# Transposes in place of identity matmuls for the input combinations, and a value group's weight sums on GpSimd

## The chip, the cores and the metric

The kernel runs on one core of a Trainium2 chip. The metric is the device time of one execution in microseconds (us). The profile is of one execution, taken by the hardware profiler. Engines are named as it names them: PE (TensorE matmuls), PEld (its weight loads), DVE (VectorE), ACT (ScalarE), POOL (GpSimd) and SP (SyncE, which issues most DMAs here). L389 is line 389 of the kernel.

## The reference

One encoder layer with two parallel gated branches is applied to two batches with the same weights: `x_prompt` (1024 rows of 1024) and `x_sample` (512 rows). The change touches the very first step for `x_prompt` alone, the normed input and its product with the columns of the input projection that give the values and the gates:

```python
def encoder_layer(x, pre_w, w_in, conv_w, conv_b, i_bias, f_bias, head_norm_w, w_pm, w_pa, w_out, post_w, rel_table):
    b_, s_, _ = x.shape
    h = rms_norm(x, pre_w)
    cols = jnp.einsum('bsd,dc->bsc', h, w_in)
    m_qk, m_v, m_o, m_z, m_i, m_f, a_qkv, a_z, gate = jnp.split(cols, np.cumsum(IN_SPLITS)[:-1], axis=-1)
    ...
    return x + rms_norm(out, post_w)
```

All is float32. What follows (a bidirectional mLSTM, dilated window attention, gated merge and output projection) is not touched.

## The kernel before

**How float32 products are made.** A float32 operand is split into a high part (rounded by an ACT copy to the matmul's faster float32 form) and a low part (DVE: value minus high part). `mm3` (L209 to L211) then makes a product of three matmuls: high by high, and the two mixed ones.

**Winograd's form of Strassen's product.** For `x_prompt` the product of input and weights is done as a two by two block product with seven block products in place of eight. The rows fall into two halves of 512 (i = 0, 1) and the 1024 input columns into two halves; `combos` (L372) calls the four blocks a0, b0 (first rows) and a1, b1 (second rows). The seven left operands are named B11, T2, B21, T3, T1, T4, B22, and kept turned (input column on the partitions) in `H[0][m]` (high) and `H[1][m]` (low), four tiles of 128x512 each. With the normed blocks: B11 = a0, B21 = b0, B22 = b1, T1 = a1 - a0, T2 = b1 - a1 + a0, T3 = b1 - a1 and T4 = b0 - b1 + a1 - a0, that is b0 - T2.

**One value group** (`value_group`, L454) covers 644 columns of the weights: `va` and `vb` hold the upper and lower half of the weights' rows, `vsum` the sums. `sums` (L444) makes three of them on DVE, 128x1288 each: vb0 + vb1, va0 - vb0 (which takes the place of vb0) and vsum0 - va0. `split` makes the high and low part of one right operand (`vhi` on ACT, L477; `vlo` on DVE, L478), into two places used in turn. `product` runs 48 matmuls of 128x322 in four groups of twelve, and between the groups it steps through a generator (`with_m1`, `with_m2`, `with_m7`, `with_m6`) in which the first group (g = 0) makes the left operands while PE multiplies. So the order on PE is written out by hand: products m1 (B11), m2 (B21), m7 (T3), m6 (T2), m5 (T1), m4 (T4), m3 (B22), and between them the puts.

**A put** (`put`, L419) makes tile k of operand m: PE turns four 128x128 blocks into one PSUM bank; ACT copies it to the high part (L432); the low part is DVE's subtraction (L434), but for B21 and B22 a matmul by the negative identity `minus` takes the high part off in PSUM (`rest`, L438) and ACT copies what is left (L439). Which blocks are turned is in `terms`: one block with the identity for B21, B22, T1 and T2 (for B21 and B22 as a plain float32 matmul, for the others as a transpose), and two blocks for T3 and T4, where the second is a plain float32 matmul by the negative identity. A plain float32 matmul of 128x128 shows as two passes in the trace, a transpose as one.

**What else runs then.** DVE norms the rows (L410, 128x512, the row block times its root and the norm weights; sixteen of them behind one another for b0, b1, a1, a0) and makes T1 and T2 in place of a0 and b1 (`sub`, L415 and L417). POOL makes the roots (L297 to L298, L406 to L407) and one half of the first low part. ACT copies the gate columns of finished value tiles (L503, `gall`) after DVE has added them up (L594, into `u2b`). DVE, ACT and POOL run their instructions in the order in which the scheduler put them; `issue_after` adds an order, and `high_priority` lets `split` go ahead. The rows and weights of the first group come by SP's queue at the start; for the groups 1 to 3 `value_group` loads `va` and `vb` as their places come free, and the results leave by SP's queue through `vz` (three places, L509 and L510).

**The later units** (`unit_pair`, L693) use the same seven left operands for the other columns.

Of the kernel before, what the change touches and what calls it, by code (L numbers as in the profile page):

```python
# [22 lines left out]
F32 = mybir.dt.float32  # L23
F32R = mybir.dt.float32r
AF = mybir.ActivationFunctionType
# [4 lines left out]
P = 128  # L30
# [15 lines left out]
VW = 322  # L46
# [135 lines left out]
class Net:  # L182
# [32 lines left out]
    def put(self, key, out, src, of, queue=None, lag=None):  # L215
        if self.defer:
            self.pending.append((self.clock + (lag or self.lag), key, (out, src), self.owner.get(id(of))))
        else:
            (queue or self.nc.sync).dma_start(out, src)
# [149 lines left out]
            self.nc.scalar.mul(self.cw[:, c], self.cw[:, c], x)  # L369


    def combos(self, ps, H, xt, r, junk, pw, minus, again, diag):  # L372

        nc = self.nc
        part = lambda i, j: [x[:, j * BLK:(j + 1) * BLK] for x in xt[i]]  # L380
        a0, b0, a1, b1 = part(0, 0), part(0, 1), part(1, 0), part(1, 1)
        plus, neg = self.ident, minus.bitcast(F32)
        terms = {B21: [(b0, plus)], B22: [(b1, plus)], T3: [(b1, plus), (a1, neg)],
                 T1: [(a0, plus)], T2: [(b1, plus)], T4: [(b0, plus), (b1, neg)]}

        def lead():
            ps_ = [ps.tile([P, BLK], F32, name="d") for _ in range(4)]
            for t in range(4):
                nc.vector.tensor_scalar(diag[t], self.ident, self.root(xt[0][t], r[t], junk), None, op0=OP.mult)  # L389
                for k in range(4):  # L390
                    nc.tensor.matmul(ps_[k][:, t * P:(t + 1) * P], a0[t][:, k * P:(k + 1) * P], diag[t], start=t == 0,
                                     stop=True, skip_group_check=True)
            for k in range(4):
                hi, lo, w = H[0][B11][:, k], H[1][B11][:, k], self.prew[:, k:k + 1]
                self.high = nc.scalar.activation(hi, ps_[k], AF.Copy, scale=w)
                self.low = nc.vector.scalar_tensor_tensor(lo, ps_[k], w, hi.bitcast(F32), op0=OP.mult, op1=OP.subtract)  # L396

        roots = {}

        def norm(i, t, j):  # L400

            if i and j and t % 2 == 0:
                two = r[4 + t // 2].rearrange("p (a b) -> p a b", a=3)
                for a in range(2):
                    nc.scalar.activation(junk, xt[i][t + a], AF.Square, accum_out=two[:, 0, a:a + 1])
                nc.gpsimd.tensor_scalar(two[:, 1], two[:, 0], 1.0 / D, EPS, op0=OP.mult, op1=OP.add)  # L406
                nc.gpsimd.tensor_tensor(two[:, 2], two[:, 1], self.mhalf, op=OP.pow)  # L407
                roots.update({t: two[:, 2, :1], t + 1: two[:, 2, 1:]})
            x, c = xt[i][t], slice(j * BLK, (j + 1) * BLK)
            return nc.vector.scalar_tensor_tensor(x[:, c], x[:, c], roots[t] if i else r[t][:, 2:3], pw[:, c], op0=OP.mult, op1=OP.mult)  # L410

        def sub(m):
            for t in range(4):
                if m == T1:
                    nc.vector.tensor_sub(a0[t], a1[t], a0[t])  # L415
                else:
                    nc.vector.tensor_sub(b1[t], b1[t], a0[t])  # L417

        def put(m, k):  # L419

            if m == T4 and k == 0:
                again()
            p = ps.tile([P, BLK], F32, name="d")
            for t in range(4):
                for i, (x, one) in enumerate(terms[m]):
                    of, to = x[t][:, k * P:(k + 1) * P], p[:, t * P:(t + 1) * P]
                    if i == 0 and m not in (B21, B22):
                        nc.tensor.transpose(to, of, one)
                    else:
                        nc.tensor.matmul(to, of, one, start=t == i == 0, stop=True, skip_group_check=True)  # L430
            hi, lo = H[0][m][:, k], H[1][m][:, k]
            nc.scalar.activation(hi, p, AF.Copy)  # L432
            if m not in (B21, B22):
                self.low = nc.vector.tensor_sub(lo, p, hi.bitcast(F32))  # L434
                return None

            def rest():
                nc.tensor.matmul(p, minus, hi, start=False, stop=True, skip_group_check=True)  # L438
                nc.scalar.activation(lo, p, AF.Copy)  # L439
            return rest  # L440

        return lead, norm, sub, put

    def sums(self, wa, wb, s):  # L444

        nc = self.nc
        nc.vector.tensor_add(s[:, 0], wb[:, 0], wb[:, 1])
        nc.vector.tensor_sub(wb[:, 0], wa[:, 0], wb[:, 0])
        nc.vector.tensor_sub(s[:, 1], s[:, 0], wa[:, 0])

    def value_weights(self, sb):
        return [sb.tile([P, 2, 4 * VW], F32, name=x, bufs=1) for x in ("va", "vb", "vsum")]
# [1 line left out]
    def value_group(self, g, T, H, sb, us, co, ps, late=None, begin=None, u3=None, more=None, turn=None):  # L454
# [4 lines left out]
        nc = self.nc  # L459
# [61 lines left out]
        if g == 0:  # L521
# [44 lines left out]
            def with_m7():  # L566
                put(T1, 0), put(T1, 1)
                yield
                put(T1, 2), put(T1, 3)
                with self.tc.issue_after(low[1]):  # L570
                    sub(T2)
                yield
                put(T2, 0), put(T2, 1)
                yield
                put(T2, 2), put(T2, 3)
                low.append(self.low.ins)
                yield

# [6 lines left out]
            for t in range(4):  # L585
                nc.scalar.activation(u2[t], m1[t][:, :VW], AF.Copy)
            w12 = low.pop(0)
            with self.tc.issue_after(low[0]):
                self.sums(wa, wb, s)
            m2 = product(B21, w12, with_m2())  # L590
            held = []
            for t in range(4):
# [3 lines left out]
                sub(T1)  # L596
            m7 = product(T3, split(wb[:, 0]), with_m7())
            for t in range(4):
                add(u3[t], u2[t], m7[t][:, :VW])
            with self.tc.issue_after(low[1]):  # L600
                s2 = split(s[:, 1])
            m6 = product(T2, s2, with_m6())
# [5 lines left out]
            yield  # L608
            co = co()
        else:  # L610
            self.sums(wa, wb, s)
            m1 = product(B11, split(wa[:, 0], first))
            for t in range(4):
                nc.scalar.activation(u2[t], m1[t][:, :VW], AF.Copy)
            w12 = split(wa[:, 1])
# [15 lines left out]
            u3 = []  # L631
            for t in range(4):
                u3.append(tile_("u3", 4))
                add(u3[t], u2[t], m7[t][:, :VW])
            yield
        if g == 0:
            with self.tc.issue_after(low[2]):
# [55 lines left out]
    def unit_pair(self, weights, H, sb, cp, ps):  # L693
# [19 lines left out]
        nc.vector.tensor_add(q[0][0], u2, m2)  # L713
        nc.vector.tensor_add(u2, u2, m6)
        m7 = product(T3, s3)
        nc.vector.tensor_add(u3, u2, m7)
        m5 = product(T1, s1)
        nc.vector.tensor_add(q[1][1], u3, m5)
        nc.vector.tensor_add(u2, u2, m5)
# [1036 lines left out]
def body(tc, a):  # L1756
    N = Net(tc, a)
    nc = tc.nc
    (x1, y1), (x2, y2) = a["runs"]
    with ExitStack() as st:  # L1760
# [12 lines left out]
        with ExitStack() as s1:  # L1773
# [4 lines left out]
            with ExitStack() as sv:  # L1778
# [37 lines left out]
                def again():  # L1816
                    H[0][T4] = place("h", T4)

                turns = N.combos(ps, H, xt, r, H[1][T4][:, :2].rearrange("p a c -> p (a c)"), pw, minus, again, diag)
# [235 lines left out]
```

## Time and profile before

| | us |
|---|---|
| median of 3 runs (2253.35 to 2256.43) | 2254.23 |
| the profiled execution | 2252.45 |
| its span, first to last instruction | 2250.7 |
| PE busy in the span | 2238.9 |
| DVE busy | 1510.2 |
| ACT busy | 1128.0 |
| POOL busy | 713.5 |

A row of the time line gives the start and the length in us, engine, line, operation, output<-inputs, the shapes and how many instructions the row stands for; in brackets the idle time of the engine before it and what ended it. In a group's row "min/median/max" are lengths in nanoseconds. In a row of the waits stand the total, the number and the longest of the waits in us. A matmul's length overlaps the next one's, so that costs on PE are read from start to start. In the kernel's first 67 us the trace has 64 passes at L428, 64 at L430 by `minus` and 64 at L430 by the identity.

### The profile page before, as it was taken

How to read it: one execution, taken by the hardware profiler on the slowest of the kernel's cores; microseconds unless marked ns; L12 is line 12 of the kernel's file. 1: busy time of each engine (PE TensorE's matmuls, PEld its weight loads, DVE VectorE, ACT ScalarE, POOL GpSimd, SP SyncE). 2: the span in 40 equal slices, each digit the busy share in tenths (PEclk: the TensorE clock that was granted, in tenths of full speed). 3: DMA queues.
4: the chain of work that ended last, by engine and by line, in shares of the span. 5: the costliest groups of instructions: out<-in, count | busy, mean ns of one | idle time of the engine just before them, and what ended most of it. 6: DMA issues, size and time to landing. Idle time of an engine off the chain costs nothing.

```text
span 2250.7 us, 35392 instructions
## 1 busy us (share of the span) xinstructions
PE 2238.9 (99%) x12226; PEld 1964.4 (87%) x12226; DVE 1510.2 (67%) x2875; ACT 1128.0 (50%) x2369; POOL 713.5 (32%) x1000
## 2 busy tenths in 40 slices
PE   9999999999999999999999999999999999999998
PEld 8999888888888888888888899999888888888887
DVE  7765577687776665558887754544689854655674
ACT  6432244444443443457776655666665644554332
POOL 1000333333333222237676610011165522221221
PEclk9999999999999999999999999999999999999999
DMA  3652455543233223284664788997678897776663
GB/s 123 172 131 76 174 202 192 195 178 120 107 111 112 85 84 131 104 294 167 224 212 133 202 213 231 257 254 212 202 244 285 253 269 222 232 258 199 225 236 114
DMA packets 222685, 418.27 MB, mean 186 GB/s; under 512 B 24841, under 2 KB 128969, under 8 KB 222506
## 3 DMA queue, kind: packets, MB, share of 16 engines
q1 hardware_dynamic: 194536, 315.86, 44.3%
q0 software_dynamic: 24368, 87.56, 12.4%
q10 hardware_dynamic: 3602, 12.59, 1.4%
q8 instruction: 97, 1.59, 0.3%
q14 instruction: 82, 0.67, 0.1%
HBM read 296.19 MB, written 128.12 MB: 189 GB/s over the span
## 4 chain that ended last, share of the span: by engine, by line
PE 97%; issue 1%; DMA 1%; DVE 0%; ACT 0%; POOL 0%; DVEq 0%; POOLq 0%; ACTq 0%
PE d L211 14%; PE d L209 14%; PE d L210 14%; PE dense L209 12%; PE dense L211 12%; PE dense L210 12%; PE o L1400 4%; PE pt L1387 2%; PE lg L1364 2%; PE num L209 1%; PE num L211 1%; PE num L210 1%; PE a L1072 1%; PE kv L209 1%; PE kv L210 1%
## 5 line engine op out<-in xcount | busy, mean ns | idle before, releaser
L209 PE MATMUL dense<-H,wh 128*128 128x512 f32 x664 | 270.3, 407 | 0.0
L211 PE MATMUL dense<-H,wl 128*128 128x512 f32 x664 | 260.6, 393 | 0.0
L210 PE MATMUL dense<-H,wh 128*128 128x512 f32 x664 | 260.4, 392 | 0.0
L210 PE MATMUL d<-Hl,phla 128*128 128x512 f32 x608 | 236.5, 389 | 0.0
L211 PE MATMUL d<-Hh,phla 128*128 128x512 f32 x608 | 236.5, 389 | 0.0
L209 PE MATMUL d<-Hh,phla 128*128 128x512 f32 x608 | 236.5, 389 | 0.0
L278 DVE TENSOR_TENSOR wl<-wraw,wh 128x1024 fp32r<-128x1024 f32 (+1 forms) x121 | 149.5, 1236 | 66.4 <-ACT wh L272 66.3
L1376 DVE CUSTOM_DVE_ANT_0 ls<-lg,bias 128x256 f32<-128x256 f32 (+1 forms) x288 | 93.7, 362 | 135.2 <-PE lg L1364 69.8
L211 PE MATMUL d<-Hh,phlb 128*128 128x512 f32 x456 | 177.4, 389 | 0.0
L209 PE MATMUL d<-Hh,phlb 128*128 128x512 f32 x456 | 177.4, 389 | 0.0
L210 PE MATMUL d<-Hl,phlb 128*128 128x512 f32 x456 | 177.4, 389 | 0.0
L1380 ACT ACTIVATE ls<-ls,nm 128x256 f32<-128x256 f32 (+1 forms) x288 | 129.9, 452 | 83.3 <-DVE nm L1378 58.2
L687 POOL TENSOR_TENSOR psum_w<-pw_raw 128x512 f32<-128x512 f32 x38 | 55.0, 1447 | 366.0 <-DMA pw_raw<-w_in 222.5
L272 ACT ACTIVATE wh<-wraw 128x1024 fp32r<-128x1024 f32 (+1 forms) x124 | 128.5, 1037 | 72.4 <-PE dense L210 26.4
L211 PEld LDWEIGHTS dense<-H,wl 128*128 128x128 f32 x664 | 124.7, 188 | 28.1
L209 PE MATMUL d<-vhi,Hh 128*128 128x322 f32 x448 | 140.9, 314 | 0.3
L211 PE MATMUL d<-vhi,Hl 128*128 128x322 f32 x448 | 140.3, 313 | 0.4 <-DVE Hl L396 0.2
L210 PE MATMUL d<-vlo,Hh 128*128 128x322 f32 x448 | 139.6, 312 | 0.0
L210 PEld LDWEIGHTS dense<-H,wh 128*128 128x128 f32 x664 | 125.3, 189 | 14.3
L209 PEld LDWEIGHTS dense<-H,wh 128*128 128x128 f32 x664 | 125.0, 188 | 14.4
L209 PEld LDWEIGHTS d<-Hh,phla 128*128 128x128 f32 x608 | 114.1, 188 | 23.7
L210 PEld LDWEIGHTS d<-Hl,phla 128*128 128x128 f32 x608 | 114.1, 188 | 23.7
(570 smaller groups left out, 6158.5 us busy)
## 6 DMA issues: line engine op xcount, KB each, us to landing
pw_raw<-w_in SPq DMA_DIRECT2D x76, 512.0 KB
wraw<-w_in SPq DMA_DIRECT2D x64, 512.0 KB
aqk_a<-pwk SPq DMA_DIRECT2D x48, 512.0 KB
aqk_b<-sw SPq DMA_DIRECT2D x48, 256.0 KB
wraw<-w_pm POOLq DMA_DIRECT2D x24, 512.0 KB, 5.8
wraw<-w_out POOLq DMA_DIRECT2D x24, 512.0 KB, 3.9
wraw<-w_v POOLq DMA_DIRECT2D x22, 430.0 KB, 6.1
erep<-erow SPq DMA_DIRECT2D x16, 512.0 KB
```

Source lines behind the costliest of these rows:

```text
L209: nc.tensor.matmul(out, lh, rh, start=start, stop=False)
L210: nc.tensor.matmul(out, lh, rl, start=False, stop=False)
L211: nc.tensor.matmul(out, ll, rh, start=False, stop=stop)
L272: high = nc.scalar.activation(hi[:, :n], raw[:, :n], AF.Copy)
L278: low = (self.lows or nc.vector).tensor_sub(lo[:, :n], raw[:, :n], hi[:, :n].bitcast(F32))
L687: self.nc.gpsimd.tensor_add(s[:, 0], ws[1][:, 0], ws[1][:, 1])
L1072: nc.tensor.matmul(p[:, c - c0], kT[:, ct, c * P:(c + 1) * P], qT[:, ct, c * P:(c + 1) * P], start=ct == 0, stop=ct == 1)
L1364: nc.tensor.matmul(lg[:, hh, c:c + w], q[hh][:, qs], z[:, k0:k0 + w], start=z is k[hh], stop=z is not k[hh])
L1376: nc.vector.tensor_tensor_reduce(out=ls[:, hh], in0=ts["lg"][hh], in1=bt[:, hh], scale=1.0, scalar=NEG, op0=OP.add, op1=OP.max, accum_out= ...
L1380: self.held = self.held[-3:] + [nc.scalar.activation(ls[:, hh], ls[:, hh], AF.Exp, bias=nm[:, hh:hh + 1], accum_out=ot[:, 128 + hh:129 + hh])]
L1387: nc.tensor.transpose(pp[:, hh * nk + x], ts["ls"][:, hh, x * P:(x + 1) * P], self.ident)
L1400: nc.tensor.matmul(po[:, hh * 64:hh * 64 + 64], pt[:, hh * nk + x], v[:, kt[x], c0 + hh * 64:c0 + hh * 64 + 64], start=x == 0, stop=x == n ...
```

## The change

- `put` turns B21, B22, T1, T2 and now T3 (a1 alone) by transposes; the second block of T3 and all of T4 come from operands that are there already, by 128x512 matmuls with the identity or its negative: T3 = a1 - B22 (high and low, two matmuls), T4 = B21 - T2 (four matmuls, no transpose). T3 has the other sign than before, so that the results of its product are subtracted (also in `unit_pair`). A copy of the identity in the fast float32 form, `plus`, is made by ACT at the start.
- T2's puts stand one place earlier (one, two and one between the groups of m7 in place of two and two).
- The three sums of the first group go from DVE to POOL and no longer wait for the norms (`issue_after` is gone).
- In the later groups the split of `va` stands before the sums in the text.

```diff
-        plus, neg = self.ident, minus.bitcast(F32)
-        terms = {B21: [(b0, plus)], B22: [(b1, plus)], T3: [(b1, plus), (a1, neg)],
-                 T1: [(a0, plus)], T2: [(b1, plus)], T4: [(b0, plus), (b1, neg)]}
+        turned = {B21: b0, B22: b1, T3: a1, T1: a0, T2: b1}
+        others = {T3: [(B22, minus)], T4: [(B21, plus), (T2, minus)]}
...
             p = ps.tile([P, BLK], F32, name="d")
-            for t in range(4):
-                for i, (x, one) in enumerate(terms[m]):
-                    of, to = x[t][:, k * P:(k + 1) * P], p[:, t * P:(t + 1) * P]
-                    if i == 0 and m not in (B21, B22):
-                        nc.tensor.transpose(to, of, one)
-                    else:
-                        nc.tensor.matmul(to, of, one, start=t == i == 0, stop=True, skip_group_check=True)
+            begun = m in turned
+            for t in range(4) if begun else ():
+                nc.tensor.matmul(p[:, t * P:(t + 1) * P], turned[m][t][:, k * P:(k + 1) * P], self.ident, is_transpose=True,
+                                 start=t == 0, stop=True, skip_group_check=True)
+            for of, one in others.get(m, ()):
+                for x in range(2):
+                    nc.tensor.matmul(p, one, H[x][of][:, k], start=not begun, stop=True, skip_group_check=True)
+                    begun = True
...
-    def sums(self, wa, wb, s):
-
-        nc = self.nc
-        nc.vector.tensor_add(s[:, 0], wb[:, 0], wb[:, 1])
-        nc.vector.tensor_sub(wb[:, 0], wa[:, 0], wb[:, 0])
-        nc.vector.tensor_sub(s[:, 1], s[:, 0], wa[:, 0])
+    def sums(self, wa, wb, s, on):
+
+        on.tensor_add(s[:, 0], wb[:, 0], wb[:, 1])
+        on.tensor_sub(wb[:, 0], wa[:, 0], wb[:, 0])
+        on.tensor_sub(s[:, 1], s[:, 0], wa[:, 0])
...
                     sub(T2)
+                put(T2, 0)
                 yield
-                put(T2, 0), put(T2, 1)
+                put(T2, 1), put(T2, 2)
                 yield
-                put(T2, 2), put(T2, 3)
+                put(T2, 3)
...
-            with self.tc.issue_after(low[0]):
-                self.sums(wa, wb, s)
+            self.sums(wa, wb, s, nc.gpsimd)
...
-                add(u3[t], u2[t], m7[t][:, :VW])
+                nc.vector.tensor_sub(u3[t], u2[t], m7[t][:, :VW])
...
-            self.sums(wa, wb, s)
-            m1 = product(B11, split(wa[:, 0], first))
+            w11 = split(wa[:, 0], first)
+            self.sums(wa, wb, s, nc.vector)
+            m1 = product(B11, w11)
...
-        nc.vector.tensor_add(u3, u2, m7)
+        nc.vector.tensor_sub(u3, u2, m7)
...
-                minus = H[1][T4][:, 3, :P]
+                minus, plus = (H[1][T4][:, 3, i * P:(i + 1) * P] for i in range(2))
...
                 nc.scalar.activation(minus, N.ident, AF.Copy, scale=-1.0)
+                nc.scalar.activation(plus, N.ident, AF.Copy)
```

Below, "a sum", "a norm", "a put", "a rest", "a split" and "the gate copy" are meant as named above; the lines are those of the kernel before. In the changed kernel as built, POOL runs the three sums behind the roots, as its next work; DVE's order is the ten last norms, the first subtraction of T1, the first sum into `u2b` (L594), then the other three subtractions of T1; ACT's order at B22 is two high copies, the split of `vb`, the gate copy (L503), two high copies and then the low copies.

More of the change, by code (lines that the diff above doesn't have):

```diff
@@ L369, in halved, with combos @@
             self.nc.scalar.mul(self.cw[:, c], self.cw[:, c], x)
-    def combos(self, ps, H, xt, r, junk, pw, minus, again, diag):
+    def combos(self, ps, H, xt, r, junk, pw, plus, minus, again, diag):
         nc = self.nc
@@ L633, in value_group @@
                 u3.append(tile_("u3", 4))
-                add(u3[t], u2[t], m7[t][:, :VW])
+                nc.vector.tensor_sub(u3[t], u2[t], m7[t][:, :VW])
             yield
@@ L1817, in again @@
                     H[0][T4] = place("h", T4)
-                turns = N.combos(ps, H, xt, r, H[1][T4][:, :2].rearrange("p a c -> p (a c)"), pw, minus, again, diag)
+                turns = N.combos(ps, H, xt, r, H[1][T4][:, :2].rearrange("p a c -> p (a c)"), pw, plus, minus, again, diag)
                 values = [N.value_group(0, A, H, vw, us, co, ps, None, (*begin, turns), [x[:, :VW] for x in xt[0]])]
```

## The prediction

> **What bounds the kernel now.** I read the page first, then the waits of TensorE (PE), then the stretches of ten microseconds over the part that the change touches, then the time lines of PE, VectorE (DVE), ScalarE (ACT) and GpSimd (POOL) there.
>
> ```profile
> PE 2238.9 (99%) x12226; PEld 1964.4 (87%) x12226; DVE 1510.2 (67%) x2875; ACT 1128.0 (50%) x2369; POOL 713.5 (32%) x1000
> ...
> PE 97%; issue 1%; DMA 1%; DVE 0%; ACT 0%; POOL 0%; DVEq 0%; POOLq 0%; ACTq 0%
> ```
> ```profile
> PE d L438 <- ACT Hh L432: 0.5, 1, 0.5
> ...
> PE d L211 <- DVE Hl L434: 0.2, 1, 0.2
> ```
> ```profile
> 20.00:30.00 10.00, 9.54 (x72) 9.10 (x71) 9.88 (x14) 7.03 (x15) 0.74 (x1) 1.00 0.00 0
> ```
>
> PE sets the end: 97% of the chain is PE's, and from 30 to 2243 us it hardly stops. So a pass taken from PE is worth its own length, as long as nothing makes PE wait there, and any new wait of PE is paid in full. The columns of the last row are the stretch, its length, and the busy time of PE, its weight loads, DVE, ACT and POOL. From 20 to 30 us, where the moved sums would run, DVE has 9.88 of 10 us of work, POOL 0.74.
>
> **PE passes removed.** Matmuls are pipelined, so I cost them from start to start.
>
> ```profile
> 27.51 1.95 PE L430 MATMUL d<-ident,x 128*128 128x128 f32 x16
> 29.21 0.39 PE L209 MATMUL d<-vhi,Hh 128*128 128x322 f32 x1
> ...
> 32.76 0.72 PE L438 MATMUL d<-Hh,Hl 128*128 128x512 f32 x2
> 33.31 0.31 PE L209 MATMUL d<-vhi,Hh 128*128 128x322 f32 x1
> ...
> 35.09 0.27 PE L428 MATMUL d<-ident,x 128*128 128x128 f32 x1
> ...
> 36.34 0.71 PE L438 MATMUL d<-Hh,Hl 128*128 128x512 f32 x2
> ...
> 42.57 0.39 PE L209 MATMUL d<-vhi,Hh 128*128 128x322 f32 x1
> ...
> 44.48 1.03 PE L428 MATMUL d<-ident,x 128*128 128x128 f32 x8
> ...
> 45.27 0.39 PE L209 MATMUL d<-vhi,Hh 128*128 128x322 f32 x1
> ```
> ```profile
> 2243.67 0.39 PE L210 MATMUL dense<-Q,K 128*128 128x512 f32 x1
> 2243.90 0.39 PE L211 MATMUL dense<-Q,K 128*128 128x512 f32 x1
> ```
>
> - B21 and B22, eight puts: two puts as plain matmuls by the identity take 29.21 - 27.51 = 1.70 us (16 passes); two puts as transposes, as T1's now, 45.27 - 44.48 = 0.79. Saved: 0.91 a pair, 1.8 for B22, 1.8 for B21. At B21 PE already waits for ACT's copy (L438, 0.5 us), and each put still needs two copies of ACT, so I count 0.5 there.
> - T3, four puts: now 36.34 - 35.09 = 1.25 (four transposes, eight passes by the negative identity). After: 0.40 of transposes and two 128x512 passes. Such a pass takes 2243.90 - 2243.67 = 0.23 in the dense part and (33.31 - 32.76)/2 = 0.275 here; I take 0.25. So 0.90, saved 0.35 x 4 = 1.4.
> - T4, four puts: the same 1.25 now; after, four 128x512 passes, 1.0. Saved 1.0 (0.6 to 1.3 by the two prices).
>
> Sum: 0.5 + 1.8 + 1.4 + 1.0 = 4.7 us less, if nothing waits. The sign of T3 costs nothing: `tensor_sub` stands where the add stood, one for one. The extra ACT copy of the identity comes before the first rows land, when ACT waits for them anyway.
>
> **The sums on GpSimd.** Here I part from the 4.7.
>
> ```profile
> 11.89 1.59 POOL L478 TENSOR_TENSOR vlo<-va,vhi 128x644 fp32r<-128x644 f32 x1 [0.93 <-ACT vhi L477]
> ...
> 19.65 1.09 POOL L407 TENSOR_TENSOR xr<-xr,mhalf 128x2 f32<-128x2 f32 x1
> ```
> ```profile
> 20.30 1.50 DVE L478 TENSOR_TENSOR vlo<-va,vhi 128x1288 fp32r<-128x1288 f32 x1
> 21.71 6.71 DVE L410 SCALAR_TENSOR_TENSOR x<-x,xr,Hh 128x512 f32<-128x512 f32 x10
> 28.34 1.50 DVE L447 TENSOR_TENSOR vsum<-vb 128x1288 f32<-128x1288 f32 x1
> 29.75 1.29 DVE L415 TENSOR_TENSOR x<-x,x 128x512 f32<-128x512 f32 x2
> 30.95 0.48 DVE L594 TENSOR_TENSOR u2b<-u,d 128x322 f32<-128x322 f32 x1
> ```
>
> On DVE a sum of 1288 columns takes 29.75 - 28.34 = 1.41 us. On POOL none is seen; 644 columns take 1.59, so 1288 some 3.18, and three sums 9.5. They no longer wait for the norms: POOL is free at 19.65 + 1.09 = 20.74 and the weights have landed (the 20 to 30 us row above has no DMA at all). With nothing in their way the sums would be ready by 30.4 us, ahead of DVE's today. But in just that time DVE does the ten norms of L410, each with two operands in SBUF. What POOL and DVE do to each other then is seen later in the trace:
>
> ```profile
> 342.17 3.05 DVE L774 SCALAR_TENSOR_TENSOR pwk<-c,pwk 128x1024 fp32r<-128x1024 f32 x1
> 343.39 2.93 POOL L688 TENSOR_TENSOR psum_w<-psum_w,pw_raw 128x512 f32<-128x512 f32 x1
> ...
> 346.29 1.29 POOL L690 TENSOR_TENSOR pw_raw<-pw_raw 128x512 f32<-128x512 f32 x1
> ...
> 346.62 2.04 DVE L669 TENSOR_TENSOR phla<-pw_raw,phla 128x1024 fp32r<-128x1024 f32 x1
> ```
> ```profile
> L669 DVE TENSOR_TENSOR phla<-pw_raw,phla x38: 1210/1220/2061, 235.0 to 936.8; 128x1024 fp32r<-128x1024 f32 x38
> ```
>
> POOL's 512 columns take 1.29 when DVE works from PSUM. Begun under L774, which reads two SBUF operands, they take 2.93: L774 ends at 345.22 and POOL 1.10 later. The other way round, L669 (median 1.22) started under POOL's L690, which ends at 347.58; it ends at 348.66, 1.08 later. So the two take turns by whole instructions, and of a POOL instruction all but the first 0.19 us shuts DVE out. A sum therefore holds DVE for 3.18 - 0.19 = 3.0 us, and DVE gets one norm (0.67) in between.
>
> [...]
>
> DVE after the change, from 20.30: split until 21.71; sum 24.7; norm 25.4; sum 28.4; norm 29.1 (the last that B22 needs); sum 32.1; eight norms 37.5; L415 (1.20/2) 38.1; L594 38.6 us. Today L594 ends at 31.43, sums included. Who waits:
>
> ```profile
> 32.64 0.22 ACT L503 ACTIVATE gall<-u2b 128x16 f32<-128x16 f32 x1
> 33.04 0.60 ACT L432 ACTIVATE Hh<-d 128x512 fp32r<-128x512 f32 x1 [0.18 <-PE d L430]
> 33.53 1.08 ACT L439 ACTIVATE Hl<-d 128x512 fp32r<-128x512 f32 x2
> ```
>
> - PE reaches B22 at 27.51 - 0.5 = 27.0 and waits 2.1 us for the norm at 29.1. Then two puts, twelve products (44.48 - 42.57 = 1.91), two puts with two rests (0.79 + 0.55), twelve products and T3's first transposes (0.40): 35.45.
> - T3's new passes read B22's low half, a copy of ACT. In the built program ACT's queue has the gate copy of L503 ahead of it, which waits for L594, and behind that two high and then the low copies. From 38.6: gate copy 38.8, two copies 39.8, low half 40.4. PE waits 40.4 - 35.45 = 4.95 us. Today T3 reads the rows themselves, so that ACT's order there hurt nobody.
> - From 40.4: T3's passes 0.5, rests 0.55, a put 0.9, twelve products 1.91, two puts 1.8: the product with T3 starts at 46.1, not 42.57: +3.5. Its low halves are then ready one step ahead, as now. T1 and T2 are put as today (T2's puts only change places, and DVE's subtraction for the first, four times 0.6 behind T3's last low half at 47.8 and a split, ends at 51.6, when PE comes to it at 51.5), T4 gives back 1.0: +2.5.
>
> What a wait of 4.95 us does to PE's clock:
>
> ```profile
> 6.81 5.90 PE L391 MATMUL d<-u2b,x 128*128 128x128 f32 x32 [0.67 <-DVE u2b L389]
> ```
> ```profile
> 10.00:11.00 1.00, 1.00 (x6) 1.00 (x6) 0.02 (x2) 0.61 (x2) 0.74 (x2) 1.00 1.00 410
> 11.00:12.00 1.00, 1.00 (x11) 1.00 (x10) 1.00 (x2) 0.81 (x2) 0.11 (x1) 1.00 1.03 422
> ```
> ```profile
> 2243.50:2246.90 3.40, 0.79 (x4) 0.32 (x2) 1.80 (x4) 0.69 (x2) 0.55 (x1) 1.00 0.38 143
> 2246.90:2250.30 3.40, 0.00 (x0) 0.00 (x0) 0.38 (x1) 0.00 (x0) 0.00 (x0) 0.50 0.41 154
> ```
>
> After PE's end the granted clock (1.00, then 0.50) falls behind a stretch of 3.4 us with 0.79 of work, that is 2.6 idle. At the start PE runs at half pace (6 passes a microsecond, then 11) from 6.81 to about 11.1, 4.3 us. So 4.95 idle most likely halves the clock, and 4.3 us at half pace lose 2.1 (bounds 0, and 3.4 for 6.8 us). [...]
>
> **The rest.** Groups 1 to 3 split their plain weights first in the text; in the built program of group 1 DVE still has the three sums ahead of that split, and groups 2 and 3 keep their order. PE has no wait there now: nothing. SP's queue has three stores of v between the two halves of the next weights and one more ahead of vb; two things keep that harmless:
>
> ```profile
> 82.80 1.27 ACT L477 ACTIVATE vhi<-va 128x1288 fp32r<-128x1288 f32 x1
> ...
> 94.34 0.47 ACT L509 ACTIVATE vz<-x 128x322 fp32r<-128x322 f32 x1 [2.42 <-DMA vs_a<-vz]
> ```
> ```profile
> 88.33 0.31 PE L209 MATMUL d<-vhi,Hh 128*128 128x322 f32 x1
> ```
>
> the split is at 82.80, far behind the load, and PE's first product of the group at 88.33. But ACT now has three more copies for stores ahead of that split, the last of which runs at 94.34 today, waiting for stores. I cost it at nothing because the first three copies move ahead to T4's puts, near 60 us, so that their stores go before vb's load instead of behind it.
>
> Sum: +2.5 + 2.1 = 4.6 on 2252.45 (the profiled execution; its span is 2250.7) = 2257.05. The median of the runs lies 2254.23 - 2252.45 = 1.78 higher: **2258.8 us**. All below is on the median's scale.
>
> **Rivals.**
> 1. The two engines take turns but PE's clock holds: +2.5, 2256.7. For it: no wait inside the kernel shows a fall, the longest is 0.6. Against: the rows at the end. [...]
> 2. **Not slower**: POOL and DVE run side by side. Then DVE, 4.2 us lighter, has L594 done by 30 us, PE never waits for it, and the 4.7 stand: 2249.5. It decides if a norm beside a sum on POOL keeps its 0.67. Against it are the rows at 343 and 346 us; for it, that no pair of 128x1288 and L410 is seen.
> 3. The stores are as late as today: ACT's split for group 1 goes from 82.80 to 94.8, its end to 96.1, so PE waits 7.8 us at 88.33, against which a lateness of 4.6 counts: 2258.8 + 3.2 = 2262.0.
> 4. The change does less than it says: PE is held by ACT's copies at every put, so that transposes save nothing, and POOL is harmless: within 1 us of 2254.2.
>
> **Numbers.** Chances: forecast 0.45 (2257 to 2260.5 by the clock's bounds), rival 1 0.25, rival 2 0.15, rival 3 0.10, rival 4 0.05. The range of 8 in 10 takes the first two, most of rival 2 and the start of rival 3: 2249.3 to 2262. A measurement of this kernel tells 0.2% (4.5 us) from no change: below 2249.7 faster, above 2258.7 slower. Slower: 0.33 of the forecast's 0.45, 0.02 of rival 1's 0.25 and all of rival 3, together 0.45; faster: 0.12 of rival 2's 0.15; the same is what is left, 0.43.
>
> **What would show it.** Right: POOL's three sums at 3 to 4.5 us each from 21 to 32 us, two of DVE's norms at some 3.7 us instead of 0.75, the gate copy ending an idle stretch of ACT near 38.7, two waits of PE of about 2 and 5 us in the waits view (B22 by DVE, T3 by ACT), and the 48 products behind T3 starting near 46. The clock: 12 products taking 3.8 instead of 1.91 in the first microseconds behind the wait. Wrong: norms of 0.75 beside the sums, or T3's put before 36 us; then rival 2. A PE wait near 90 us is rival 3.

## The result and the profile after

The changed kernel takes 2258.83 us (median of 11 runs, 2255.14 to 2260.90); the kernel before, in 11 runs beside it, 2253.36 (2252.22 to 2256.43). The ratio is 1.0020, with a 95% interval of 1.0011 to 1.0029: slower by some 5.5 us. The profiled execution of the changed kernel took 2260.11 us. Nearly all of the loss stands in the first 100 us. The waits view of PE (total, number and longest, in us) of the changed kernel:

```profile
PE d L429 <- ACT Hl L439: 4.3, 1, 4.3
...
PE d L210 <- DVE vlo L477: 1.3, 1, 1.3
PE d L425 <- DVE x L409: 1.3, 1, 1.3
PE d L209 <- ACT vhi L476: 1.0, 1, 1.0
```

Between 20 and 100 us no wait of PE was longer than 0.5 us before. Now there are four of 1 us and more. Two stand at T3 (L429, a wait for ACT's low copy) and B22 (L425, a wait for a norm); the other two, on `vlo` and `vhi`, are at the start of the second value group. The same kernel in stretches of ten microseconds (start and end, length, busy time of PE, its weight loads, DVE, ACT and POOL, granted clock, DMA share, GB/s):

```profile
20.00:30.00 10.00, 7.75 (x50) 6.50 (x49) 10.00 (x4) 6.69 (x15) 9.92 (x4) 1.00 0.00 0
30.00:40.00 10.00, 5.67 (x35) 5.05 (x34) 10.00 (x15) 3.47 (x8) 0.84 (x1) 0.87 0.00 1
40.00:50.00 10.00, 10.00 (x56) 9.18 (x55) 5.86 (x9) 5.08 (x11) 0.00 (x0) 0.79 0.01 2
```

From 20 to 40 us DVE and, to 31, POOL are busy without a gap, and PE is not. From 37 to 44 us the granted clock is down (0.87 and 0.79 are means over stretches with 1.00 and 0.50). Now the time line of POOL, DVE and ACT there:

```profile
20.25 3.87 POOL L446 TENSOR_TENSOR vsum<-vb 128x1288 f32<-128x1288 f32 x1
24.20 3.27 POOL L447 TENSOR_TENSOR vb<-va,vb 128x1288 f32<-128x1288 f32 x1
27.43 3.41 POOL L448 TENSOR_TENSOR vsum<-vsum,va 128x1288 f32<-128x1288 f32 x1
```
```profile
21.26 14.77 DVE L409 SCALAR_TENSOR_TENSOR x<-x,xr,Hh 128x512 f32<-128x512 f32 x10
...
36.55 0.48 DVE L593 TENSOR_TENSOR u2b<-u,d 128x322 f32<-128x322 f32 x1
```
```profile
37.06 0.23 ACT L502 ACTIVATE gall<-u2b 128x16 f32<-128x16 f32 x1 [6.37 <-DVE u2b L593]
37.19 1.07 ACT L432 ACTIVATE Hh<-d 128x512 fp32r<-128x512 f32 x2
38.14 1.09 ACT L439 ACTIVATE Hl<-d 128x512 fp32r<-128x512 f32 x2
```

The ten norms took 6.71 us before and take 14.77 beside the three sums, 2.7 us more for each sum: three of the ten last 3.42 to 3.44 us, the other seven 0.74. DVE's first sum into `u2b` starts at 36.55 instead of 30.95, and ACT, which had nothing else in the way, sat idle for 6.37 us in front of the gate copy, with B22's last copies behind it. On PE:

```profile
33.98 0.48 PE L429 MATMUL d<-Hh,Hl 128*128 128x512 f32 x1
38.79 0.79 PE L429 MATMUL d<-Hl,Hl 128*128 128x512 f32 x1 [4.33 <-ACT Hl L439]
...
43.82 0.47 PE L210 MATMUL d<-vlo,Hh 128*128 128x322 f32 x1
44.09 0.41 PE L211 MATMUL d<-vhi,Hl 128*128 128x322 f32 x1
44.34 0.31 PE L209 MATMUL d<-vhi,Hh 128*128 128x322 f32 x1
44.49 0.30 PE L210 MATMUL d<-vlo,Hh 128*128 128x322 f32 x1
```

T3's first put uses B22's high part at once and then waits 4.33 us for the low part. Behind the wait the products stand 0.27 us apart until 44.09, and 0.15 apart from 44.34: half clock. The second value group, on ACT, DVE and PE:

```profile
58.90 1.15 ACT L508 ACTIVATE vz<-u2b 128x306 fp32r<-128x306 f32 x3
...
70.78 0.46 ACT L508 ACTIVATE vz<-u2b 128x306 fp32r<-128x306 f32 x1 [3.61 <-DMA vs_a<-vz]
...
90.08 0.48 ACT L508 ACTIVATE vz<-x 128x322 fp32r<-128x322 f32 x1 [2.28 <-DMA vs_a<-vz]
90.46 1.26 ACT L476 ACTIVATE vhi<-va 128x1288 fp32r<-128x1288 f32 x1
```
```profile
91.99 1.49 DVE L477 TENSOR_TENSOR vlo<-va,vhi 128x1288 fp32r<-128x1288 f32 x1
```
```profile
91.78 0.41 PE L209 MATMUL d<-vhi,Hh 128*128 128x322 f32 x1 [1.00 <-ACT vhi L476]
93.54 0.41 PE L210 MATMUL d<-vlo,Hh 128*128 128x322 f32 x1 [1.35 <-DVE vlo L477]
```

The first copies for the stores go early, at 58.90, but the fourth waits until 70.78 for one of the three places in `vz`, and the later ones wait again. The high part of the next `va` is made at 90.46, behind a copy of a finished tile that waited for a place in `vz`, that is for an earlier store to land. It was made at 82.80 before, behind seven copies for stores; now eleven stand ahead of it.

To place gains and losses I use two distances, each from the first product of m1 (its first `vhi` matmul at L209; 48 matmuls a product, so that each product's first one can be counted off): to the first of m5, which lies behind B22, T3 and T4, and to the first of the second product of the second group, which lies behind the late split. Before, they are 53.90 and 82.76 us. In the changed kernel they are 56.74 and 88.38: 2.84 lost by m5, 2.78 more at the second group, 5.62 in all. The medians below follow the second distance to within 2.5 us. The stage from the first matmul into `dense` (which comes between 963 and 977 us) to the end of PE's work, which no part of the change touches, takes between 1273.6 and 1279.0 us in the profiles of this study, so that a single profile's total says little about 2 us.

### The profile page after: what moved, and what is told of

Same layout as the page of the kernel before. It is cut to its first block, busy times and chain, and to the rows that moved or that the text cites. A ratio compares the mean times of both kernels' runs of the same rounds, so it can differ in the third digit from the quotient of the medians.

```text
span 2258.3 us, 35206 instructions
## 1 busy us (share of the span) xinstructions
PE 2236.6 (99%) x12138; PEld 1957.9 (87%) x12138; DVE 1513.6 (67%) x2872; ACT 1128.9 (50%) x2370; POOL 729.7 (32%) x1003
## 3 DMA queue, kind: packets, MB, share of 16 engines
q8 instruction: 96, 1.57, 0.3%
## 4 chain that ended last, share of the span: by engine, by line
PE 93%; DMA 2%; DVE 2%; issue 1%; ACT 1%; POOL 0%; SPq 0%; DVEq 0%; POOLq 0%; ACTq 0%
PE d L210 13%; PE d L211 13%; PE d L209 13%; PE dense L209 12%; PE dense L211 12%; PE dense L210 12%; PE o L1400 4%; PE pt L1387 2%; PE lg L1364 2%; PE num L209 1%; PE num L211 1%; PE num L210 1%; PE a L1072 1%; PE kv L209 1%; PE kv L210 1%
## 5 line engine op out<-in xcount | busy, mean ns | idle before, releaser
L209 PE MATMUL dense<-H,wh 128*128 128x512 f32 x664 | 270.6, 408 | 1.2 <-DVE V0b L1645 0.7
L209 PE MATMUL d<-Hh,phla 128*128 128x512 f32 x608 | 236.5, 389 | 0.0
L687 POOL TENSOR_TENSOR psum_w<-pw_raw 128x512 f32<-128x512 f32 x38 | 59.6, 1568 | 371.5 <-DMA pw_raw<-w_in 345.9
L209 PE MATMUL d<-Hh,phlb 128*128 128x512 f32 x456 | 177.4, 389 | 0.0
L209 PE MATMUL d<-vhi,Hh 128*128 128x322 f32 x448 | 140.9, 315 | 1.3 <-ACT vhi L476 1.0
L209 PEld LDWEIGHTS dense<-H,wh 128*128 128x128 f32 x664 | 125.1, 188 | 16.8 <-DVE mg L1713 1.3
L209 PEld LDWEIGHTS d<-Hh,phla 128*128 128x128 f32 x608 | 114.1, 188 | 23.7
```

Of the source, the lines that this page charges most:

```text
L209: nc.tensor.matmul(out, lh, rh, start=start, stop=False)
L687: self.nc.gpsimd.tensor_add(s[:, 0], ws[1][:, 0], ws[1][:, 1])
```

## The experiments

Each kernel is the one before or the changed one with the edit shown. All ran with the kernel before beside them (medians 2253.61, 2253.21 and 2254.10 in the three sets). The last two columns are the two distances against the kernel before, from one profile each.

| | median, us | ratio to before (95%) | to m5 | to group 2 |
|---|---|---|---|---|
| changed kernel | 2258.83 | 1.0020 (1.0011 to 1.0029) | +2.84 | +5.62 |
| e1_sums_on_dve | 2252.12 | 0.9995 (0.9986 to 1.0003) | -5.12 | -1.65 |
| e2_only_sums | 2257.12 | 1.0019 (1.0010 to 1.0028) | +3.06 | +3.03 |
| e4_idle_gpsimd | 2259.85 | 1.0025 (1.0015 to 1.0034) | +4.94 | +7.01 |
| e11_gpsimd_writes | 2252.43 | 0.9992 (0.9983 to 1.0002) | -5.15 | -3.71 |
| e12_one_source_norms | 2258.64 | 1.0021 (1.0012 to 1.0030) | +2.37 | +5.88 |
| e5_filled_wait | 2255.51 | 1.0012 (1.0003 to 1.0021) | +1.03 | +3.54 |
| e6_gate_copy_later | 2255.14 | 1.0006 (0.9997 to 1.0015) | -0.45 | +1.10 |
| e10_after_early_split | 2253.59 | 1.0001 (0.9992 to 1.0010) | +2.78 | +2.68 |
| e8_sums_behind_split | 2251.84 | 0.9993 (0.9984 to 1.0002) | -5.17 | -3.86 |
| e7_stores_on_gpsimd | 2247.53 | 0.9973 (0.9963 to 0.9983) | -5.12 | -5.23 |
| e9_early_split | 2245.96 | 0.9968 (0.9956 to 0.9981) | -5.14 | -5.24 |

**The passes alone, and the sums alone.** e1 takes the sums back, e2 moves nothing but them.

```diff
-            self.sums(wa, wb, s, nc.gpsimd)
+            with self.tc.issue_after(low[0]):
+                self.sums(wa, wb, s, nc.vector)
```

> The changed kernel, but the first group's three sums are back on DVE behind the norms, as before the change. Turn-taking theory: the ten norms take about 6.7 us again, PE has no wait over 1 us at B22 and T3, the granted clock stays at 1.00 from 20 to 60 us, and m5's first product starts 4.7 us earlier than in the kernel before (62.0 instead of 66.7, or 0.3 less where the profile's axis begins later, as in the changed kernel). ACT's queue at the second group is as in the changed kernel, so the 2.8 us lost there (from m5 to the group's second product 31.6 us instead of 28.9) are lost again: 2253.4 - 4.7 + 2.8 = 2251.5. Rival, the sums on GpSimd cost nothing and the loss lies in the new passes: products as late as in the changed kernel, about 2258. Rival, the loss at the second group came from the lateness at T3: no loss there, 2248.7.

For e2, in the kernel before (with `sums` taking the engine as in the changed one):

```diff
-            with self.tc.issue_after(low[0]):
-                self.sums(wa, wb, s)
+            self.sums(wa, wb, s, nc.gpsimd)
```

> The kernel before with one edit, its first three sums on GpSimd and not held behind the norms. Turn-taking theory: the ten norms take about 14.8 us instead of 6.7, DVE's first sum into u2b ends near 37 instead of 31.4, ACT's gate copy waits for it and PE waits for the norm at B22 (1 to 1.6 us) and for ACT's copies behind the gate copy (about 2 us), too short for a fall of the clock: 2253.4 + 3.5 = 2257 (2255.5 to 2260). Side by side: the norms stay at 6.7 us, no new wait of PE, 2253 or up to 1 us less.

DVE in e1, then DVE, ACT and PE in e2:

```profile
21.32 6.71 DVE L409 SCALAR_TENSOR_TENSOR x<-x,xr,Hh 128x512 f32<-128x512 f32 x10
```
```profile
21.24 14.79 DVE L410 SCALAR_TENSOR_TENSOR x<-x,xr,Hh 128x512 f32<-128x512 f32 x10
```
```profile
37.66 0.23 ACT L502 ACTIVATE gall<-u2b 128x16 f32<-128x16 f32 x1 [6.80 <-DVE u2b L592]
```
```profile
38.42 0.99 PE L438 MATMUL d<-Hh,Hl 128*128 128x512 f32 x2 [1.77 <-ACT Hh L432]
```

With the sums on DVE the norms are back at 6.71, PE has no wait at B22 and T3, and m5 comes 5.12 us earlier than before: that is the worth of the passes. At the second group 3.5 of it is lost again (48.78 to 81.11 us, against 53.90 to 82.76), so that the time hardly moves. With only the sums moved, the norms take 14.79 and 3 us are lost, as expected, but not quite where expected: B22's norm holds PE for 0.20 us (1 to 1.6 were foreseen), and B22's rests then wait 1.77 us on ACT. T3 reads the rows themselves here, and the clock holds (1.00 from 20 to 60 us). So the loss does not need the new passes.

**Is it GpSimd's work, or what the sums' results are used for?** e4 adds to e1 four additions that nobody waits for; e11 puts memsets in their place.

```diff
+            for _ in range(4):
+                nc.gpsimd.tensor_add(junk, w[:, :1024], w[:, 200:1224])
```

> e1_sums_on_dve with four GpSimd additions of 128x1024 float32 behind the roots, from the weights into a free place that nobody reads: work that nobody waits for. Turn-taking theory: each takes about 2.6 us alone and shuts DVE out for 2.2 to 2.4 us, so the ten norms beside them take 15.5 to 16.5 us instead of 6.7, DVE's chain down to the low half of vb ends some 9 us later, and PE, that has no link with these additions, waits 4 to 8 us at B22 and at the product with T3; time 4 to 8 us above e1_sums_on_dve. Side by side: norms 6.7 us, the same time as e1_sums_on_dve.

```diff
-            for _ in range(4):
-                nc.gpsimd.tensor_add(junk, w[:, :1024], w[:, 200:1224])
+            for _ in range(12):
+                nc.gpsimd.memset(junk.bitcast(F32), 0.0)
```

> e4_idle_gpsimd with twelve memsets of 128x1024 in the place of the four additions: GpSimd is as busy beside the norms (some 12 us, about 1 us each by the small memsets of the profile before), but it only writes SBUF. Theory of the shared read path: the ten norms take 6.7 us as without them, and the time is that of e1_sums_on_dve, 2251 to 2253. Rival, any work of GpSimd in SBUF shuts DVE out: norms of 14 us or more and 2257 to 2260.

POOL and DVE in e4, then in e11:

```profile
21.18 11.71 POOL L444 TENSOR_TENSOR Hl<-va 128x1024 fp32r<-128x1024 f32 x4
```
```profile
22.18 15.23 DVE L409 SCALAR_TENSOR_TENSOR x<-x,xr,Hh 128x512 f32<-128x512 f32 x10
```
```profile
21.80 12.10 POOL L444 MEMSET Hl<- 128x1024 f32 x12
```
```profile
22.82 6.71 DVE L409 SCALAR_TENSOR_TENSOR x<-x,xr,Hh 128x512 f32<-128x512 f32 x10
```

Four additions hold DVE for (15.23 - 6.71)/4 = 2.1 us each (just under what was expected), and PE, which has no link with them, loses 10 us by m5 against e1 and the run 7.7 us. Two falls of the clock, of 3.41 us each, are part of that. Twelve microseconds of memsets cost DVE nothing (6.71 us for the ten norms, as in e1). So it is not enough that POOL is busy, nor that it writes SBUF: what the additions do and the memsets do not is to read it and to add, and no run parts the two. A read path that both engines share, the theory of the expectation, fits these times; the path itself is not shown.

**One operand in DVE's norms.** e12 is the changed kernel without the multiplication by the norm weights in the sixteen last norms.

```diff
-            return nc.vector.scalar_tensor_tensor(x[:, c], x[:, c], roots[t] if i else r[t][:, 2:3], pw[:, c], op0=OP.mult, op1=OP.mult)
+            return nc.vector.tensor_scalar(x[:, c], x[:, c], roots[t] if i else r[t][:, 2:3], None, op0=OP.mult)
```

> The changed kernel, its sixteen last norms as tensor_scalar by the row's root alone; the multiplication by the norm weights is left out of them, so that DVE reads one operand from SBUF in place of two. Theory of the shared read path: the sums on GpSimd (3.2 us each) no longer shut the norms out; the ten norms take 6.7 us or less, PE has no wait over 1 us at B22 and T3, m5 starts 48.8 us or less behind the first product, time 2251 to 2253 with the loss at the second group. Rival, any work of DVE in SBUF takes turns with GpSimd: norms of 12 to 15 us and 2257 to 2260.

```profile
17.61 0.88 DVE L409 TENSOR_SCALAR x<-x,xr 128x512 f32<-128x512 f32 x2 [0.87 <-POOL xr L406]
...
21.34 12.11 DVE L409 TENSOR_SCALAR x<-x,xr 128x512 f32<-128x512 f32 x10
```

The rival won, and my theory fell in the form in which I had put it. Ten such norms would take about 4.0 us alone (two take 0.88 in the first row, each 0.48 long, so that they start 0.40 us apart), so that each sum holds DVE for (12.11 - 4.0)/3 = 2.7 us, as with two operands. A second operand in SBUF is therefore not needed for DVE to be held. The two forms differ in pace too: the new one does 512 columns in 0.40 us, the old one in 0.66 (start to start). Why the norms with one operand are held as long is not shown.

**The clock.** e5 fills the wait at T3 with PE work.

```diff
+            if m == T3 and k == 0:
+                for _ in range(14):
+                    nc.tensor.matmul(p, minus, H[0][B11][:, 0], start=True, stop=True, skip_group_check=True)
```

> The changed kernel with fourteen extra 128x512 passes (about 3.5 us, their result overwritten by the transposes that follow) ahead of T3's first put, in the place of most of its 4.3 us wait. Clock theory: PE stays busy, the granted clock stays at 1.00 from 20 to 60 us, the wait at T3 shrinks to about 1 us but ends at the same time as before, and the products behind T3 run at 0.15 us at once; m5 starts about 2.3 us earlier against the kernel's first product (54.4 us behind it, not 56.7), time 2258.8 - 2.3 = 2256.5. Rival, the clock did not cost anything (the lost time lies in other waits): m5 stays at 56.7 us, about 2259, or more for the extra passes.

```profile
34.62 3.34 PE L426 MATMUL d<-Hh,Hl 128*128 128x512 f32 x14
...
39.83 0.50 PE L432 MATMUL d<-Hl,Hl 128*128 128x512 f32 x1 [1.20 <-ACT Hl L442]
```
```profile
30.00:40.00 10.00, 8.80 (x54) 7.80 (x53) 10.00 (x14) 3.62 (x8) 1.87 (x1) 1.00 0.00 1
40.00:50.00 10.00, 9.84 (x63) 8.68 (x64) 7.70 (x12) 6.09 (x13) 0.00 (x0) 1.00 0.01 2
```

ACT's low copy comes no sooner (39.17 us, with the ten norms from 22.29, against 38.14 and 21.26), the clock stays at 1.00, and m5 comes 1.8 us earlier than in the changed kernel (54.93 against 56.74). PE does more work and the kernel is faster. The fall of the clock was real and cost 2.5 us at T3's product (31.76 us behind m1's instead of 34.23), of which 1.8 are left by m5 in these profiles; the medians differ by 3.3, and their intervals (each 2 us to either side) can't tell the two apart.

**The queue of ACT.** e6 moves the gate copies behind B22's low copies.

```diff
-                nc.scalar.activation(lo, p, AF.Copy)
+                self.rest_end = nc.scalar.activation(lo, p, AF.Copy)
...
-                nc.scalar.activation(self.gates_of(T, blk * 4 + t), ...
+                with self.tc.issue_after(self.rest_end.ins):
+                    nc.scalar.activation(self.gates_of(T, blk * 4 + t), ...
```

> The changed kernel, but ACT's gate copies stand behind B22's low copies in its queue. Queue theory: B22's copies no longer wait for the norms, T3's first put goes ahead near 34 us; the next put then waits for the bank that DVE's first sum into u2b frees near 37 us, so one wait of about 2 us is left in the place of 4.3, too short for a fall of the clock, and T3's product starts near 41.5 instead of 46.6: 2258.8 - 5 = 2254 (2252.5 to 2255.5). Rival, DVE's lateness holds PE by itself, whatever ACT's order: no gain, 2258 to 2259.

```profile
38.23 0.66 PE L425 MATMUL d<-ident,x 128*128 128x128 f32 x4 [1.95 <-DVE u2b L594]
```

T3's first put goes ahead, and the second waits 1.95 us for the bank that DVE's sum frees: both as expected. T3's product starts 29.27 us behind m1's, not 34.23; by m5, 3.29 is left of these 4.96, because T3's last high copies now stand behind a later gate copy and a split in ACT's queue (PE waits 0.72 us for them, among others). The clock stays at 1.00 in this profile, so that the 4.96 us hold both the shorter wait (1.95 instead of 4.33) and the fall that does not come. DVE's lateness reaches PE by two ways, and ACT's order was the longer one.

**The second group.** Two edits on e1: the first group's values are split for the stores on GpSimd (e7), the sums of the later groups are held behind the split (e8), or both (e9). e10 has both in the changed kernel.

```diff
-                nc.scalar.activation(z[:, 0, :w], x, AF.Copy)
-                nc.vector.tensor_sub(z[:, 1, :w], x, z[:, 0, :w].bitcast(F32))
+                if g == 0:
+                    nc.gpsimd.tensor_copy(z[:, 0, :w], x)
+                else:
+                    nc.scalar.activation(z[:, 0, :w], x, AF.Copy)
+                (nc.gpsimd if g == 0 else nc.vector).tensor_sub(z[:, 1, :w], x, z[:, 0, :w].bitcast(F32))
...
-            self.sums(wa, wb, s, nc.vector)
+            with self.tc.issue_after(self.splits[1].ins):
+                self.sums(wa, wb, s, nc.vector)
```

> e1_sums_on_dve with two edits at the second group: the first group's copies and subtractions for the stores run on GpSimd instead of ACT and DVE, so that ACT's split of the next weights has nothing ahead of it that waits for a store, and DVE's sums of the later groups are held behind that split. Queue theory: PE no longer waits at the second group (from m5's first product to the group's second product 28.9 us as in the kernel before), 2.8 us less than e1_sums_on_dve, about 2248.7, the best so far. Rival, PE waits there for the weights' own load: the same time as e1_sums_on_dve.

> e1_sums_on_dve with one of the two edits of e9_early_split: DVE's sums of the later groups are held behind the split, while ACT and DVE still make the first group's stores. Queue theory: ACT's copy of the weights still stands behind three copies that wait for stores, so the second group still starts late: 2251 to 2252.5, within 1 us of e1_sums_on_dve. Rival, the sums on DVE were what held the split: 2246 to 2247, as e9_early_split.

> e1_sums_on_dve with the other one of the two edits of e9_early_split: the first group's copies and subtractions for the stores run on GpSimd, and the sums of the later groups stay where they were in DVE's queue. Queue theory (what blocks the split is ACT's queue, behind copies that wait for stores): the group's second product starts 28.8 to 29.5 us behind m5's first, not 32.3, and the time is within 1 us of e9_early_split: 2246 to 2247. Rival, both edits are needed (DVE's sums hold the low half once ACT's half comes early): 2249 to 2251.

> The changed kernel (sums of the first group on GpSimd) with both edits of e9_early_split. Sum-of-parts theory: the loss at T3 stays (m5 2.8 us later than in the kernel before, against the first product), the loss at the second group (2.8 us) goes: 2258.8 - 2.8 = 2256. Rival, the lateness at T3 would have been taken up at the second group anyway: no gain, 2258.8. Rival, the two losses share the clock's fall: 2254 or less.

ACT in e8, then in e9:

```profile
81.47 0.47 ACT L508 ACTIVATE vz<-x 128x322 fp32r<-128x322 f32 x1 [3.04 <-DMA vs_a<-vz]
81.85 1.27 ACT L476 ACTIVATE vhi<-va 128x1288 fp32r<-128x1288 f32 x1
```
```profile
76.36 1.28 ACT L476 ACTIVATE vhi<-va 128x1288 fp32r<-128x1288 f32 x1 [5.92 <-PE d L211]
```

What held the second group is ACT's queue. In e8 the split still stands behind a copy that waits for a store; in e9 it waits only until PE is done with its place, at 76.36, and PE has no wait there. e7 alone gives all of it (28.75 us from m5 to the group's second product, as before: 28.86) and e8 next to nothing in the median; in its profile 1.3 us are lost there, about as many as in e11's (1.4), which has e1's order of work. e9 and e7 beat both kernels: e9 by 7.65 us in 2253.61, 0.9968. They keep the passes' gain, 5.1 us, and lose nothing later. The medians give more than the 5.2 of the second distance, by 1 to 2.5 us; the intervals hold that difference, and I leave it open. They also hold the 1.57 us between e7 and e9, where at most 1 was expected. In the changed kernel the same edits give 2.9 us by the second distance (88.38 to 85.44) and 5.2 in the median, where 2.8 was expected: again more than the profile shows, and within the two intervals. What brought the four further copies ahead of the split is not shown: no run takes back the new order in the text of the later groups alone. e2, which has neither that order nor the new passes, keeps seven copies ahead of the split and loses nothing there (+3.06 at m5, +3.03 at the second group).

## Why the prediction was right, point by point

The time was predicted as 2258.8 us and is 2258.83. The mechanism of the first 60 us was right; that the number fits to 0.1 us is luck: the loss by m5 was forecast 1.8 us too large, the loss at the second group, 2.8 us, was put at nothing, and the offset was taken 0.9 too large.

- **Turns of POOL and DVE: right**, shown by e1, e2, e4 and e11. The sums last 3.87, 3.27 and 3.41 us in the time line (3 to 4.5 foreseen), and each holds DVE for 2.7 us, not 3.0. I had taken 3.18 - 0.19 from the 644 columns of 1.59. The other row of the same profile, 512 columns in 1.10 us once the way is free, would have given 1.10 x 1288/512 = 2.8.
- **Who waits: right.** B22 by DVE, T3 by ACT behind the gate copy, which ended ACT's idle stretch at 37.06 (38.7 foreseen, on an axis whose first product comes 0.45 us later). Sizes: 1.33 and 4.33 us, where I had 2.1 and 4.95; of the difference of 1.4 us, three times 0.3 is the shorter hold of the sums. What does not stand is that DVE's second operand is what matters: e12 has one and is held as long.
- **The passes: 5.1 us instead of 4.7**, by e1. B21 gave 0.84 (12.06 us from m1's to m2's first product, before 12.90) where I counted 0.5 for fear of ACT. T4's four passes take 0.90 to 0.93 from start to start where I took 1.0.
- **The clock: right that it falls**; it cost 1.8 us by m5 (e5), with 2.1 predicted. That the size came near is in part luck: 5.5 us behind the wait were at half clock (38.79 to 44.30), where I took 4.3, and e5 shows 2.5 at T3's product, of which 0.7 were made up by m5. No row of the profile before shows the upper bound of 6.8 us at half clock; in the changed kernel the clock was at half for 6.8 us (37.47 to 44.30), the first 1.3 of them inside the wait.
- So by m5 the forecast had +4.6 and the profile shows +2.84. Of these 1.8 us, 1.1 stand at T3's product (34.23 us behind m1's, before 29.76: +4.47, where 3.5 + 2.1 were foreseen) and the rest between it and m5.
- **The step that failed** is the last one: "I cost it at nothing because the first three copies move ahead to T4's puts, near 60 us, so that their stores go before vb's load instead of behind it." The copies did move (58.90 us), and their stores did go before vb's load (issued from 63.12 us, the load at 74.00). But the fourth copy sat until 70.78 for a store to land, and the split came at 90.46, with 1.00 and 1.35 us of waits behind it: 2.78 us, by the mechanism of rival 3 (the split behind copies that wait for stores), which I gave 0.10, though not by its condition, since the stores came earlier than before. Its price there was 3.2. The error was to look at the first copies and to stop there: the split stands behind eleven copies (four more than before, where I had counted three more), with three places for them, and it is the last copy ahead of it that decides.
- **The offset.** I added 1.78 us for the median over the profiled execution, from three runs. Eleven runs give 2253.36 - 2252.45 = 0.91. So 2252.45 + 2.84 + 2.78 + 0.91 = 2258.98, where the forecast had 2252.45 + 4.6 + 0 + 1.78. This sum is no proof of the parts: the profile of the changed kernel took 2260.11, which is 2.0 more than 2252.45 + 5.62, and the stage behind the first matmul into `dense` alone was 2.3 us longer in it (1278.0 against 1275.7).
- **Rival 2** (side by side) is out by the norms' 14.77 us. **Rival 1** (the clock holds) is out by the granted clock of this profile; by an estimate from the rows at the end, a wait of 4.33 us leaves at most 3.41 - 4.33/2 = 1.25 us of work in one of the windows of 3.41 us that it touches, and 1.21 brought a fall, so that other executions with such a wait should show it too. How long it lasted in them is not shown; their mean granted clocks run from 0.997 to 0.999, the two fastest having 0.999. **Rival 4** is out by e1: the passes save what they should.
- That the later groups' sums keep their place although the split stands first in the text was right for the second group: DVE made them ahead of `vlo` (91.99 us), and e8, which does hold them back, shows that this place costs next to nothing.
- T2's puts, one place earlier, were not tried by themselves.

## What to carry to other kernels

Before work goes to GpSimd "because it is idle", look at what DVE does in that stretch: here each of the sums and additions on GpSimd, which read SBUF, took 2.1 to 2.7 us out of DVE's work on operands in SBUF, be it two (e4) or one (e12), while the memsets, which only write it, took nothing (e11). Passes saved on the bounding engine are worth little until what feeds its next stage comes earlier too: in e1 the saving was there (5.1 us), and a copy queue that waits for stores took most of it back, until those copies moved to the idle engine at a time when it hurt nobody. And where an in-order queue has an instruction that waits, price the last thing ahead of the one you need, not the first.

## What the runs showed of the hardware

**The clock fell behind windows of 3.41 us that were only half idle.** In these profiles the changes of the granted clock inside the kernel lie a whole number of 3.41 us apart: at 37.47 and 44.30 us in the changed kernel, at 39.28, 42.69, 49.52 and 52.93 in e4, at 85.32 and 88.73 in e1. Cut along that grid, the stretches around the falls of the changed kernel read so (columns as above; PE's busy time is the first number behind the length):

```profile
34.06:37.47 3.41, 0.40 (x3) 0.08 (x1) 3.41 (x6) 0.41 (x2) 0.00 (x0) 1.00 0.00 0
37.47:40.88 3.41, 2.09 (x7) 1.69 (x8) 3.41 (x6) 3.25 (x8) 0.00 (x0) 0.50 0.00 0
40.88:44.30 3.42, 3.42 (x13) 3.23 (x13) 1.46 (x3) 1.04 (x3) 0.00 (x0) 0.50 0.00 0
```

One window with 0.40 us of PE work brought half clock in the next one. That next one had 2.09 us of work and was followed by another at half clock: 6.8 us in all. In e4, for its second fall, and in e1 the clock fell behind windows with more work:

```profile
46.11:49.52 3.41, 1.21 (x8) 1.21 (x9) 3.41 (x6) 1.32 (x5) 0.00 (x0) 1.00 0.00 0
49.52:52.93 3.41, 3.41 (x16) 3.37 (x15) 3.41 (x5) 1.12 (x2) 0.00 (x0) 0.50 0.02 5
93.89:97.30 3.41, 1.86 (x10) 1.63 (x11) 3.41 (x7) 0.87 (x3) 0.18 (x2) 1.00 0.89 176
97.30:100.72 3.42, 3.42 (x25) 3.42 (x24) 1.00 (x4) 0.81 (x3) 0.16 (x2) 1.00 1.01 192
```
```profile
81.90:85.32 3.42, 1.87 (x11) 1.37 (x10) 3.42 (x7) 1.86 (x4) 0.00 (x0) 1.00 0.60 147
85.32:88.73 3.41, 3.41 (x15) 3.41 (x14) 1.96 (x6) 0.70 (x3) 0.34 (x2) 0.50 1.03 155
```

1.21 us of work in a window of 3.41 brought a fall; 1.87 did in e1, and 1.86 did not in e4. 0.20 in e4 (35.87 to 39.28 us) and 1.46 in e11 (1839.25 to 1842.67) brought one too, and 2.06 in the changed kernel (92.08 to 95.49) did not; in the profiles of the kernel before and the changed one no window at full clock with that much or more was followed by half clock. So in these rows the border lies near half a window, as far as PE's busy time, whose ends are modelled, can tell, and two waits of 0.43 and 1.12 us at the second group were enough for it in e1. Of the 3.5 us that e1's profile loses there, against 1.4 in e11's with the same order of work, the 3.41 us at half clock can be up to 1.7. The grid does not start with the products: the first change to full clock comes 2.20 us ahead of m1 in the changed kernel's profile and 1.65 us in that of the kernel before.

**POOL and DVE alternated one by one.** With both queues full, each sum on POOL was followed by one norm on DVE and then by the next sum: three sums started at 20.25, 24.20 and 27.43 us, three norms at 21.26, 24.60 and 27.94, and PE got its norms at that pace.
